# A two-layer encoder trunk on one Trainium2 core: other starting banks, evictions ahead of weight preparations, other memory for summed blocks and evenly spaced convolution taps

## Chip, cores and metric

The kernel runs on one core of one Trainium2 chip. The metric is the device time of one launch in microseconds, as the median of three runs. Five engines work side by side: PE (TensorE, matrix products), DVE (VectorE), ACT (ScalarE), POOL (GpSimd) and SP (SyncE), which here only issues transfers. Each takes its instructions in one fixed order. Products accumulate in banks of a separate memory (PSUM) and are read out of them by DVE or ACT, which the text calls an eviction.

## The reference, cut to what matters

```
for l in range(2):
    h = h + 0.5 * swiglu(rmsnorm(h), w_gate1, w_up1, w_down1)
    h = h + hybrid_mixer(rmsnorm(h), w_in, w_attn_out, conv_w, ..., w_conv_out, w_out)
    h = h + 0.5 * swiglu(rmsnorm(h), w_gate2, w_up2, w_down2)
out = rmsnorm(h)[:, 16:]

def swiglu(x, w_gate, w_up, w_down):
    return (silu(x @ w_gate) * (x @ w_up)) @ w_down

def hybrid_mixer(u, ...):
    q, k, v, a, b, g_sb, g_conv = split(u @ w_in)
    y_sb = stick_breaking_attention(q, k, v) @ w_attn_out
    y_conv = silu(layernorm(depthwise_conv31(a * sigmoid(b)))) @ w_conv_out
    return (sigmoid(g_sb) * y_sb + sigmoid(g_conv) * y_conv) @ w_out
```

All data are float32. There are 528 tokens (512 and 16 learned ones in front), 1024 channels, a feed-forward width of 2816, 8 heads of 64, 512 convolution channels and 31 taps. The last feed-forward stage computes 512 tokens only.

## The kernel before, in words

**Layout.** Channels lie on the 128 partitions and tokens along the free axis; the residual stream is eight tiles `h0` to `h7` of 128x528. A product of 528 columns goes to a bank pair in two halves of 264.

**Precision.** Each operand is split into a rounded high part and the rest: `wh` and `wl` for weights, `uh` and `ul`, `ah` and `al` and so on for activations. Each product is three matmuls (high-high, low-high, high-low). Preparing one weight block is therefore: a DMA into `wr`, a cast on ACT (`wh`, L80) and a subtraction on DVE (`wl`, L81). There are three `wr` buffers, so the DMA of a block starts when the block three places earlier has had its `wl` made. SP issues these transfers in order. `prep_unit` and `unit` (L200 on) run this some units ahead of the products.

**Fewer products by sums.** Two rows of blocks by two columns are multiplied with seven products instead of eight, which needs sums of weight blocks (`s1` to `s4`) and of activation blocks. Sums of raw weights are made partly by accumulating DMAs of POOL (`s<-wg`, `s<-wu`, L209, on top of a block that SP loaded) and partly by adds on DVE (L278). `fetch_sums` loads these blocks into their own tiles.

**Stages.** In each layer: feed-forward 1, mixer, feed-forward 2. Each feed-forward stage computes gate and up in groups of 128 channels, multiplies `silu(gate)` with up (`g`, then `silu` on ACT, then `up`; function `evict`, L669 to L671), splits the result into `ah` and `al`, and after each of four groups adds the down products of these channels: eight products (`down`, L306), of which each is scaled on DVE (`dt`, L803) and added to `h` on POOL (L805). The first feed-forward stage of layer 0 starts in its own way.

**Openings.** The other five stages (three feed-forward, two mixers) begin with `pair`: two sets of seven products interleaved in the order of the table `OPENING`:

```
    OPENING = (("o11", 0), ("o11", 1), ("o21", 0), ("s1", 0), ("s2", 0), ("o21", 1), ("w22", 0), ("s3", 0), ("s1", 1),
               ("s2", 1), ("s4", 0), ("s3", 1), ("w22", 1), ("s4", 1))
```

Each step is 24 matmuls on PE. Its bank tags are `ps` (two banks), `pb` and `pe` (one each); in the mixers their names read `bs`, `bb` and `be`. A step ends with work on other engines: a copy (ACT, L463 and L470), a difference with the kept copy `q` (DVE, L476) or an eviction (`take`). In the feed-forward stages `take` is `evict`; in the mixers it makes the gated convolution input `uc` (L941 to L945). The DVE add behind `s2` and `s4` stands in `prep_unit` (L278), directly ahead of the cast of the sum. After the pair of a feed-forward stage comes its first `down` group. It has four down weights of 512 columns ahead in preparation; its first two products take both `ps` banks, one of which was last used by the last product of the pair.

**The mixer after its pair.** Products `q`, `k`, `v` and the gates (L886) run between the pieces of attention; each half product is evicted on DVE (L986). The 31 taps on four channel tiles (`y`, L911 and L914, 124 instructions a layer) are put behind evictions by `conv_some`: with `CONV_STEP` 5 these are 2 for each evicted half product, and 5 for each call in the pair. What is left of them runs after the first output products of attention.

**Order.** The order on each engine is made by a scheduler from priorities in program order; `with priority(-URGENT)` moves work up, `priority(LATE)` down, and `follow` places a preparation behind the instruction that the products wait for. PE's order in the openings is written out by hand (`manual_schedule`). Memory comes from pools; the summed blocks of a mixer's opening lie in the pool `glu`, whose memory becomes free while the feed-forward stage ahead finishes.

Of the kernel before, what the change touches and what calls it, by code (L numbers as in the profile page):

```python
# [7 lines left out]
F32 = mybir.dt.float32  # L8
# [5 lines left out]
P = 128  # L14
# [47 lines left out]
def kernel(ctx, tc, hT, par, const, wg1, wu1, wd1, win, wao, wco, wout, wg2, wu2, wd2, out):  # L62
# [124 lines left out]

    fetches, later_sums = [], []
# [43 lines left out]
    def fetch_sums(count):  # L232

        for n, name in later_sums[state["sums"]:state["sums"] + count]:
            _, *at = units[n][0]
            if tuple(at[:2]) != quads["of"]:
                return
            state["sums"] += 1
            tag = "s3" if name == "s3" else "s1"
            bufs = 1 if name == "s3" and at[0] == 2 else 2  # L240
            t = quads["pool"].tile([P, 8, P], F32, tag=tag, bufs=bufs, name=tag)
            load(t, n, *{"s1": ("w11", "w12"), "s3": ("w22", "w12")}.get(name, (name,)))
            raws[(name, *at)] = t
# [8 lines left out]
    def prep_unit():  # L252
# [17 lines left out]
        else:  # L270
# [5 lines left out]
            if nk in ("s2", "s4"):  # L276
# [159 lines left out]
    def pair(ptile, sp, st, mode, of, ats, between, take, done):  # L436
# [41 lines left out]

        Bs = [ptile("pb")]
# [5 lines left out]
        for ks in (range(KH - 1), (KH - 1,)):  # L485
            for A, w in zip(As, ws):
                products(A, w, x(0, 0), True, ks)
        begin(Bs[0], v(As[0]))
        copy = ahead["act"]
        between(ptile("pe"), copy)  # L490
        Bs.append(kept(As[1], False))
        G, q, E, c22 = {}, {}, {}, {}

        def step(name, n):
            w = unit(name, *of, ats[n])
            if name == "o21":
                products(As[n], w, x(0, 1))
                take(n, As[n], 0, 0)
# [12 lines left out]
            elif name == "s3":  # L511
# [26 lines left out]
    def rsqrt(r, x, y, ps, n, eps, epscol):  # L538
# [3 lines left out]
        dve.tensor_scalar(out=x, in0=ps, scalar1=1.0 / n, scalar2=eps, op0=ALU.mult, op1=ALU.add)  # L542
# [71 lines left out]
    def ffn(l, fi, st, mode, after):  # L614
# [3 lines left out]
        with tc.tile_pool(name=f"ffn{l}{fi}", bufs=1, reuse_waits="tile") as fp, \  # L618
# [47 lines left out]
            def evict(g, u, c, t):  # L666

                s = toks[t]
                dve.tensor_tensor(out=g[:, s], in0=c[:, 0, :TH], in1=norm["r"][:, s], op=ALU.mult)  # L669
                fn(g[:, s], g[:, s], AF.Silu)  # L670
                dve.tensor_tensor(out=u[:, s], in0=c[:, 1, :TH], in1=g[:, s], op=ALU.mult)  # L671

            def head():
# [9 lines left out]
                def take(n, c, i, t):  # L683
                    if (n, i) not in gu:
                        gu[n, i] = gtile(), fp.tile([P, T], F32, tag="up", bufs=3, name="up")
                    evict(*gu[n, i], c[:, :, :TH], t)
# [99 lines left out]
            def down(gi, opened=False, tp=None):  # L786
# [21 lines left out]
                ws = [unit(f"d{fi}", l, gi, j) for j in ORDER[:2]]  # L808
# [531 lines left out]
```

## Time and profile before

| What | Value |
|---|---|
| median of 3 runs | 2160.44 us |
| the runs | 2160.3, 2160.44, 3285.61 us |
| the profiled execution | 2159.91 us |
| its span, first to last instruction | 2158.1 us |
| matmuls on PE | 16058 |
| mean granted TensorE clock | 0.996 |
| DMA | 334.34 MB |

The profiled execution is 0.5 us below the median, and 1.8 us of it lie outside the span. The profile comes in several views. The page has the busy time of each engine and the chain of work that ended last. The table of waits lists, for one engine, which of its instructions waited, on what, for how long in total, how often, and the longest one. The windows give PE's busy time, the granted clock (PEclk, 1.00 is full) and the share of the DMA engines in stretches of the span. The timeline lists single instructions with start, duration and the idle time before them. Names are those of the program with the buffer numbers left out.

### The profile page before, as it was taken

The page shows a single profiled execution, that of the slowest core. Times are in us where ns is not written, and L with a number is a line of the kernel's source. Part 1 is how long each engine was busy: PE and PEld are TensorE (multiplying, and loading weights), DVE is VectorE, ACT ScalarE, POOL GpSimd, SP SyncE. Part 2 cuts the span into 40 slices and gives each one's busy share as a digit, 9 for nine tenths or more (in the row PEclk, how much of TensorE's full clock was granted, in tenths as well). Part 3 has the DMA queues.
Part 4 walks back from the last instruction along what each step waited for, and adds up shares of the span by engine and source line. Part 5 has one row for each costly group of instructions (what it writes and reads, how often), then busy time and mean ns, then how long its engine had stood idle before and what let it go on. Part 6 is the DMA issues. An engine that isn't in the chain of part 4 may idle for free.

```text
span 2158.1 us, 40005 instructions
## 1 busy us (share of the span) xinstructions
PE 2124.5 (98%) x16058; PEld 2036.0 (94%) x16058; DVE 1595.7 (74%) x2233; ACT 1171.1 (54%) x1660; POOL 512.5 (24%) x477
## 2 busy tenths in 40 slices
PE   9999999999999999999999999999999999999998
PEld 9999999999999999999999999999888888899897
DVE  6867688977766777677787666889777768767685
ACT  6434356577776634343563433466778775444354
POOL 1322321311111231313124222213212112422220
PEclk9999999999999999999999999999999999999999
DMA  7465436765578867464376646358656788665532
GB/s 225 138 166 143 136 104 192 200 137 122 125 178 180 186 160 188 127 160 124 98 189 174 167 134 160 96 171 212 143 127 137 182 186 198 180 172 144 150 106 81
DMA packets 152121, 334.34 MB, mean 155 GB/s; under 512 B 16896, under 2 KB 21120, under 8 KB 151936
## 3 DMA queue, kind: packets, MB, share of 16 engines
q1 hardware_dynamic: 110928, 235.27, 34.3%
q0 software_dynamic: 40320, 95.96, 26.1%
q8 instruction: 126, 2.06, 0.4%
q10 hardware_dynamic: 688, 0.55, 0.1%
q14 instruction: 59, 0.48, 0.1%
HBM read 325.30 MB, written 6.42 MB: 154 GB/s over the span
## 4 chain that ended last, share of the span: by engine, by line
PE 86%; DVE 6%; DMA 4%; ACT 2%; issue 1%; SPq 0%; ACTq 0%; DVEq 0%; POOL 0%; POOLq 0%
PE pb L748 15%; PE ps L748 14%; PE ps L886 13%; PE ps L306 12%; PE ps L872 10%; PE pb L306 6%; PE pe L306 5%; PE pe L748 5%; DVE wl L81 2%; PE z L1068 1%; PE po L1112 1%; ACT wh L80 1%; PE z L1091 1%; DMA wr<-wd 1%; DVE y L914 1%
## 5 line engine op out<-in xcount | busy, mean ns | idle before, releaser
L80 ACT CAST wh<-wr 128x1024 fp32r<-128x1024 f32 (+4 forms) x296 | 263.8, 898 | 353.5 <-PE ps L306 102.1
L81 DVE TENSOR_TENSOR wl<-wr,wh 128x1024 fp32r<-128x1024 f32 (+4 forms) x296 | 326.8, 1107 | 63.2 <-ACT wh L80 60.6
L80 ACT CAST wh<-s 128x1024 fp32r<-128x1024 f32 x171 | 179.4, 1049 | 288.1 <-DVE s L278 108.9
L81 DVE TENSOR_TENSOR wl<-s,wh 128x1024 fp32r<-128x1024 f32 x171 | 233.3, 1365 | 55.8 <-ACT wh L80 55.0
L805 POOL TENSOR_TENSOR h<-h,dt 128x528 f32<-128x528 f32 (+1 forms) x96 | 178.9, 1870 | 262.6 <-DVE dt L803 262.1
L886 PE MATMUL ps<-uh,wh 128*128 128x264 f32 (+1 forms) x664 | 208.0, 313 | 2.7 <-DVE q L986 2.7
L886 PE MATMUL ps<-ul,wh 128*128 128x264 f32 (+1 forms) x664 | 203.7, 307 | 0.0
L886 PE MATMUL ps<-uh,wl 128*128 128x264 f32 (+1 forms) x664 | 203.5, 307 | 0.0
L209 POOL DMA_DIRECT2D s<-wg x81 | 71.8, 886 | 530.9 <-DMA s<-wg 229.5
L914 DVE SCALAR_TENSOR_TENSOR y<-uc,prm,y 128x528 f32<-128x528 f32 (+1 forms) x240 | 186.5, 813 | 0.5
L748 PE MATMUL ps<-ul,wh 128*128 128x264 f32 (+1 forms) x576 | 163.7, 284 | 0.0
L748 PE MATMUL pb<-sl,wh 128*128 128x264 f32 (+1 forms) x576 | 163.3, 283 | 0.0
L748 PE MATMUL ps<-uh,wl 128*128 128x264 f32 (+1 forms) x576 | 163.3, 283 | 0.0
L748 PE MATMUL pb<-sh,wl 128*128 128x264 f32 (+1 forms) x576 | 163.2, 283 | 0.0
L748 PE MATMUL pb<-sh,wh 128*128 128x264 f32 (+1 forms) x576 | 162.9, 283 | 0.0
L748 PE MATMUL ps<-uh,wh 128*128 128x264 f32 (+1 forms) x576 | 162.6, 282 | 0.0
L306 PE MATMUL ps<-ah,wh 128*128 128x264 f32 (+1 forms) x616 | 144.0, 304 | 8.4 <-DVE up L671 8.2
L306 PE MATMUL ps<-al,wh 128*128 128x264 f32 (+1 forms) x616 | 143.8, 304 | 1.0 <-DVE al L81 0.8
L306 PE MATMUL ps<-ah,wl 128*128 128x264 f32 (+1 forms) x616 | 143.4, 303 | 0.0
L263 ACT CAST wh<-wr 128x1024 fp32r<-128x1024 f32 x91 | 95.4, 1049 | 83.0 <-PE ps L886 39.9
L886 PEld LDWEIGHTS ps<-uh,wh 128*128 128x128 f32 x664 | 124.9, 188 | 8.6 <-issue 1.7
L886 PEld LDWEIGHTS ps<-uh,wl 128*128 128x128 f32 x664 | 125.0, 188 | 5.9
(404 smaller groups left out, 6840.1 us busy)
## 6 DMA issues: line engine op xcount, KB each, us to landing
wr<-wd SPq DMA_DIRECT2D x96, 384.0 KB, 3.4
wr<-wg SPq DMA_DIRECT2D x129, 256.0 KB, 3.1
wr<-wu SPq DMA_DIRECT2D x129, 256.0 KB, 3.6
wr<-win SPq DMA_DIRECT2D x56, 512.0 KB, 3.9
wl<-win POOLq DMA_DIRECT2D x54, 512.0 KB, 7.9
s<-wg SPq DMA_DIRECT2D x87, 256.0 KB, 4.5
s<-wu SPq DMA_DIRECT2D x87, 256.0 KB, 5.3
s<-wg POOLq DMA_DIRECT2D x81, 256.0 KB, 5.3
```

Of the source, the lines that this page charges most:

```text
L80: i = act.copy(hi, x)
L81: return i, dve.tensor_tensor(out=lo, in0=x, in1=f(hi), op=ALU.subtract)
L209: queue.dma_start(raw[:, a:b], src, **kw)
L263: act.copy(hi[:, :nk], raw[:, :nk])
L306: pe.matmul(ps[:, c, :n], wt[:, k0 + k, :], xt[:, s:s + n], start=(k == 0 and pi == 0), stop=(k == end and pi == 2))
L748: pe.matmul(ps[:, e, :TH], wt[:, 4 * e + kk, :], xt, start=start and kk == 0 and pi == 0, stop=kk == 3 and pi == 2, skip_group_check=True)
L805: pool.tensor_tensor(out=tri(h[j], mode), in0=tri(h[j], mode), in1=tri(t, mode), op=ALU.add)
L872: pe.matmul(ps, wt[:, k0 + k, :], xt[:, s], start=(n == 0 and pi == 0), stop=(n == nk - 1 and pi == 2))
L886: pe.matmul(ps, wt[:, k, :], xt[:, s], start=(n == 0 and pi == 0), stop=(n == KD - 1 and pi == 2))
L914: t = dve.scalar_tensor_tensor(out=y, in0=uc[i][:, c0 + k:k + T], scalar=col(w0 + k), in1=y, op0=ALU.mult, op1=ALU.add)
L1068: pe.matmul(z[:, hh, :n], kk[r, ks], qq[r, q0:q0 + n], start=(pi == 0), stop=False, skip_group_check=True)
L1091: pe.matmul(z[:, hh, pq - q0:pq - q0 + pn], onesm, s[:, hh, :], start=False, stop=False, skip_group_check=True)
```

## The change

Seven edits, all in the openings and their surroundings:

1. **The first down group of an opened feed-forward stage** (`down`): three products begin together, in the banks `ps`, `pb` and `pe`, instead of two in the two `ps` banks. None of the three was used by the last product of the pair.
2. **Evictions first** (`out` in `pair`, `done`): most evictions of the pair, and the split of their results, run under `priority(-URGENT)`, and the preparations of weights are told to follow them.
3. **The add for `s4`** (`add_w21`): it leaves `prep_unit` and is issued two steps of the pair or more ahead, at the steps `("w22", 0)` and `("s4", 0)`.
4. **The start of the pair**: the first two products interleave by their inner blocks in the pattern 0-2, 0-1, 3, 2-3, so the first of them ends six matmuls earlier.
5. **Summed blocks**: their tiles are allocated in the reverse of the order in which they are loaded, and in the mixers they come from a pool of their own (`gls`).
6. **Taps**: none is placed in the pair or behind the first `q`; behind each other half product there are 2.5 on average (a credit is carried over).
7. **Constants** of the mixer are staged in `gls` too.

```diff
@@ pair
+        def out(n, c, i, t):
+            with priority(-URGENT):
+                ahead["act"], ahead["dve"] = take(n, c, i, t)
+
...
-        for ks in (range(KH - 1), (KH - 1,)):
-            for A, w in zip(As, ws):
-                products(A, w, x(0, 0), True, ks)
+        for n, ks in ((0, (0, 1, 2)), (1, (0, 1)), (0, (3,)), (1, (2, 3))):
+            products(As[n], ws[n], x(0, 0), True, ks)
...
+        def add_w21(n):
+            x, y = raws[("s1", *of, ats[n])], raws[("w21", *of, ats[n])]
+            dve.tensor_tensor(out=x, in0=x, in1=y, op=ALU.add)
+
         def step(name, n):
+            if (name, n) in (("w22", 0), ("s4", 0)):
+                add_w21(int(name == "s4"))
             w = unit(name, *of, ats[n])
             if name == "o21":
                 products(As[n], w, x(0, 1))
-                take(n, As[n], 0, 0)
+                (out if n else take)(n, As[n], 0, 0)
...
                 opposite(c22[n], Bs[n], q[n])
-                take(n, c22[n], 1, 1)
+                out(n, c22[n], 1, 1)
             elif name == "w22":
                 products(E[n], w, sx(3))
-                take(n, E[n], 1, 0)
+                out(n, E[n], 1, 0)
             else:
                 done(n, 1)
                 products(Bs[n], w, x(1, 1))
-                with priority(-n * URGENT):
-                    take(n, Bs[n], 0, 1)
+                out(n, Bs[n], 0, 1)
                 done(n, 0)
@@ prep_unit
-            if nk in ("s2", "s4"):
+            if nk == "s2" or nk == "s4" and at not in opened:
@@ done, in the head of a feed-forward stage
                     if i:
-                        while late:
-                            parts(*late.pop())
-                        parts(u, ms[n] + 1)
+                        with priority(-URGENT):
+                            while late:
+                                parts(*late.pop())
+                            parts(u, ms[n] + 1)
@@ down
-                ws = [unit(f"d{fi}", l, gi, j) for j in ORDER[:2]]
-                pds = [ptile() for j in range(2)]
+                ws, pds = [], []
+                if opened:
+                    tags = ("ps", "pb", "pe", "ps")
+                n0 = 3 if opened else 2
+                for n in range(n0):
+                    state["look"] = LOOK - n * opened
+                    ws.append(unit(f"d{fi}", l, gi, ORDER[n]))
+                    pds.append(ptile(tags[n]))
+                state["look"] = LOOK
                 with tc.manual_schedule(engines={mybir.EngineType.PE}) if opened else nullcontext():
                     for ks in (range(nk - 2), (nk - 1,), (nk - 2,)):
-                        for j in range(2):
+                        for j in range(n0):
                             gemm(pds[j], ws[j], 0, nk, xs, mode, ks, nk - 2)
@@ fetch_sums
+        some = []
         for n, name in later_sums[state["sums"]:state["sums"] + count]:
...
+            if units[n][0][1:3] == quads["of"]:
+                some.append((n, name))
+        state["sums"] += len(some)
+        for n, name in some[::-1]:
             tag = "s3" if name == "s3" else "s1"
...
+            raws[(name, *units[n][0][1:])] = quads["space"].tile([P, 8, P], F32, tag=tag, bufs=bufs, name=tag)
+        for n, name in some:
+            load(raws[(name, *units[n][0][1:])], n, *{"s1": ("w11", "w12"), "s3": ("w22", "w12")}.get(name, (name,)))
@@ mixer
-                conv_some(CONV_STEP * sum(s.stop - s.start for _, s in outs) // HALF // 2, i)
+                conv_some(CONV_STEP * sum(s.stop - s.start for _, s in outs) / T, i)
...
             def conv_some(n, behind):
+                credit[0] += n
                 with priority(LATE):
-                    while n and todo and (todo[0][0] | 1) < len(uc):
+                    while credit[0] >= 1 and todo and (todo[0][0] | 1) < len(uc):
...
-                    conv_some(CONV_STEP, last_evac[0])
...
-                quads.update(pool=glu, of=(2, l))
+                quads.update(pool=glu, space=gls, of=(2, l))
                 if l == 0:
-                    constants(glu)
+                    constants(gls)
...
-                                conv_some(CONV_STEP * (c.stop - c.start) // HALF // 2, ev)
+                                if name != "q" or i:
+                                    conv_some(CONV_STEP * (c.stop - c.start) / T, ev)
```

The change moves instructions at three places that matter here. The first is PE at the first down group of feed-forward 2 in layer 0 (its twins in layer 1 read alike). `ps_9583`, `ps_9584` and `pb_9642` are down products, `ah_9531`, `ah_9408`, `ah_9535` and `ah_9567` the high parts of the four activation blocks, the last of which comes from the last eviction of the pair. Before:

```order
L306 MATMUL ps_9583<-ah_9408,wl_9455 128x264 x2
L306 MATMUL pb_9642<-ah_9531,wh_9525 128x264 x2
L306 MATMUL pb_9642<-al_9532,wh_9525 128x264
L306 MATMUL ps_9584<-ah_9531,wh_9492 128x264 x2
L306 MATMUL ps_9584<-al_9532,wh_9492 128x264 x2
L306 MATMUL ps_9584<-ah_9531,wl_9493 128x264 x2
```

Now, with `ah_9571` as the block from the last eviction:

```order
L308 MATMUL ps_9581<-ah_9413,wl_9459 128x264 x2
L308 MATMUL pb_9582<-ah_9535,wh_9496 128x264 x2
L308 MATMUL pb_9582<-al_9536,wh_9496 128x264 x2
...
L308 MATMUL pe_9583<-ah_9535,wh_9529 128x264 x2
L308 MATMUL pe_9583<-al_9536,wh_9529 128x264 x2
...
L308 MATMUL pe_9583<-ah_9539,wl_9530 128x264 x2
L308 MATMUL ps_9581<-ah_9571,wh_9458 128x264 x2
```

Before, 15 matmuls stood between the last product of the pair and the first matmul into the bank that this product had used (`ps_9584`). Now no bank of the three is that one, and 54 matmuls stand ahead of the first that reads `ah_9571`.

The second place is DVE in the same opening, from the step `w22` of the first set to the `s3` of the second. `s_9015` and `s_9014` hold the block that is added for `s4`. Before:

```order
L669 TENSOR_TENSOR g<-c_9327,rstd 128x264
L278 TENSOR_TENSOR wr<-wr,s_9015 128x1024
L671 TENSOR_TENSOR up<-c_9327,g 128x264
L81 TENSOR_TENSOR wl<-wr,wh 128x1024
L81 TENSOR_TENSOR wl<-s_9223,wh 128x1024
L476 SCALAR_TENSOR_TENSOR pe<-ps,q 128x264
L81 TENSOR_TENSOR al<-up,ah 128x528
L476 SCALAR_TENSOR_TENSOR pe<-ps,q 128x264
L81 TENSOR_TENSOR wl<-wr,wh 128x1024
L278 TENSOR_TENSOR s_9116<-s_9116,s_9297 128x1024
L669 TENSOR_TENSOR g<-pb,rstd 128x264
L81 TENSOR_TENSOR wl<-s_9116,wh 128x1024
```

Now, from the place of the add on `wr`:

```order
L680 TENSOR_TENSOR g<-ps,rstd 128x264
L502 TENSOR_TENSOR wr<-wr,s_9014 128x1024
L682 TENSOR_TENSOR up<-ps,g 128x264
L81 TENSOR_TENSOR wl<-wr,wh 128x1024
...
L680 TENSOR_TENSOR g<-c_9332,rstd 128x264
L502 TENSOR_TENSOR s_9120<-s_9120,s_9302 128x1024
L682 TENSOR_TENSOR up<-c_9332,g 128x264
...
L680 TENSOR_TENSOR g<-pb,rstd 128x264
L682 TENSOR_TENSOR up<-pb,g 128x264
L81 TENSOR_TENSOR wl<-s_9120,wh 128x1024
```

The add on `wr` went from the eviction of `c` to the first eviction of the pair (`g<-ps`), and the second add took its old place; where the second add was, the eviction of `pb` now runs through without it.

The third place is DVE at the end of the pair of the mixer in layer 0, from the last gated input `uc` to the first `k`. Before:

```order
L942 TENSOR_TENSOR uc_4817<-bs,rstd 128x264
L914 SCALAR_TENSOR_TENSOR y_5045<-uc_4855,prm,y_5045 128x528
L914 SCALAR_TENSOR_TENSOR y_5043<-uc_4709,prm,y_5043 128x528
...
L986 SCALAR_TENSOR_TENSOR q<-ps,rstd 128x264
L914 SCALAR_TENSOR_TENSOR y_5043<-uc_4709,prm,y_5043 128x528
```

Now:

```order
L964 TENSOR_TENSOR uc_4820<-bs,rstd 128x264
L1008 SCALAR_TENSOR_TENSOR q<-ps,rstd 128x264 x2
L81 TENSOR_TENSOR ql<-q,qh 128x528
L1008 SCALAR_TENSOR_TENSOR k<-ps,rstd 128x264
L932 TENSOR_SCALAR y_5229<-uc_4712,prm 128x528
```

Five taps stood between the last `uc` and the first `q`, and four behind it; both halves of `q` now come directly behind the last `uc`, and the taps start behind the first half of `k`.

More of the change, by code (lines that the diff above doesn't have):

```diff
@@ L185, in pieces @@
         return [(0, nk, src[:, :nk])]
+    quads["space"] = None
     fetches, later_sums = [], []
@@ L232, in fetch_sums @@
     def fetch_sums(count):
+        some = []
         for n, name in later_sums[state["sums"]:state["sums"] + count]:
[L235 to L238, printed above, removed]
+            if units[n][0][1:3] == quads["of"]:
+                some.append((n, name))
+        state["sums"] += len(some)
+        for n, name in some[::-1]:
             tag = "s3" if name == "s3" else "s1"
[L240 to L243, printed above, removed]
+            bufs = 1 if name == "s3" and units[n][0][1] == 2 else 2
+            raws[(name, *units[n][0][1:])] = quads["space"].tile([P, 8, P], F32, tag=tag, bufs=bufs, name=tag)
+        for n, name in some:
+            load(raws[(name, *units[n][0][1:])], n, *{"s1": ("w11", "w12"), "s3": ("w22", "w12")}.get(name, (name,)))
     ahead = {}
@@ L541, in rsqrt @@
         fn(r, r, AF.Exp, bias=B_ZERO, scale=-0.5)
-        dve.tensor_scalar(out=x, in0=ps, scalar1=1.0 / n, scalar2=eps, op0=ALU.mult, op1=ALU.add)
+        ahead["rstd"] = dve.tensor_scalar(out=x, in0=ps, scalar1=1.0 / n, scalar2=eps, op0=ALU.mult, op1=ALU.add)
         dve.tensor_tensor(out=y, in0=r, in1=r, op=ALU.mult)
@@ L668, in evict @@
                 s = toks[t]
-                dve.tensor_tensor(out=g[:, s], in0=c[:, 0, :TH], in1=norm["r"][:, s], op=ALU.mult)
-                fn(g[:, s], g[:, s], AF.Silu)
+                i = dve.tensor_tensor(out=g[:, s], in0=c[:, 0, :TH], in1=norm["r"][:, s], op=ALU.mult)
+                j = fn(g[:, s], g[:, s], AF.Silu)
                 dve.tensor_tensor(out=u[:, s], in0=c[:, 1, :TH], in1=g[:, s], op=ALU.mult)
+                return j, i
             def head():
@@ L685, in take @@
                         gu[n, i] = gtile(), fp.tile([P, T], F32, tag="up", bufs=3, name="up")
-                    evict(*gu[n, i], c[:, :, :TH], t)
+                    return evict(*gu[n, i], c[:, :, :TH], t)
                 def done(n, i):
@@ L805, in update @@
                     pool.tensor_tensor(out=tri(h[j], mode), in0=tri(h[j], mode), in1=tri(t, mode), op=ALU.add)
-                ws = [unit(f"d{fi}", l, gi, j) for j in ORDER[:2]]
-                pds = [ptile() for j in range(2)]
+                ws, pds = [], []
[7 more added lines that the diff above has]
+                state["look"] = LOOK
                 with tc.manual_schedule(engines={mybir.EngineType.PE}) if opened else nullcontext():
                     for ks in (range(nk - 2), (nk - 1,), (nk - 2,)):
-                        for j in range(2):
+                        for j in range(n0):
                             gemm(pds[j], ws[j], 0, nk, xs, mode, ks, nk - 2)
-                for n in range(2):
+                for n in range(n0):
                     update(ORDER[n], pds[n])
-                for n, j in list(enumerate(ORDER))[2:]:
+                for n, j in list(enumerate(ORDER))[n0:]:
                     if last and after is finish_prepare and n == KD - 2:
@@ L916, in conv_some @@
                         tc.add_manual_dep(t.ins, behind.ins.name, NOSYNC, reason="convolution in the gaps")
-                        n -= 1
+                        credit[0] -= 1
             with tc.tile_pool(name=f"glu{l}", bufs=1, reuse_waits="tile") as glu, \
+                    tc.tile_pool(name=f"gls{l}", bufs=1, reuse_waits="tile") as gls, \
                     tc.tile_pool(name=f"psg{l}", bufs=1, space=bass.MemoryType.PSUM, reuse_waits="tile") as psg:
@@ L943, in take @@
                                                      op=ALU.mult)
-                    fn(x[:, a:b], x[:, a:b], AF.Sigmoid)
+                    i = fn(x[:, a:b], x[:, a:b], AF.Sigmoid)
                     pool.tensor_tensor(out=y[:, PAD + a:PAD + b], in0=y[:, PAD + a:PAD + b], in1=x[:, a:b], op=ALU.mult)
-                    conv_some(CONV_STEP, last_evac[0])
+                    return i, last_evac[0]
                 def done(n, i):
```

4 lines of the change are left out of this document (2 added, 2 removed).

## The prediction, made before the changed kernel was run

> **What bounds the kernel now.** I read the page first, for the engine that is never idle.
>
> ```profile
> span 2158.1 us, 40005 instructions
> PE 2124.5 (98%) x16058; PEld 2036.0 (94%) x16058; DVE 1595.7 (74%) x2233; ACT 1171.1 (54%) x1660; POOL 512.5 (24%) x477
> ```
>
> PE is busy for 98% of the span, so 2158.1 - 2124.5 = 33.6 us of idle time is all that an edit to waits can give, plus whatever the clock costs. The number of matmuls stays. Next comes the table of PE's waits over the whole span (total, times, longest).
>
> ```profile
> PE ps L306 <- DVE up L671: 8.2, 3, 3.2
> PE ps L886 <- DVE q L986: 2.7, 2, 1.5
> PE ps L457 <- DVE up L671: 1.6, 1, 1.6
> PE pe L457 <- DVE pe L476: 1.4, 2, 0.9
> PE pb L457 <- DVE wl L81: 1.3, 2, 0.6
> PE ps L306 <- DVE al L81: 0.8, 2, 0.4
> PE bb L457 <- DVE wl L81: 0.8, 1, 0.8
> PE bs L457 <- ACT bb L470: 0.4, 2, 0.2
> ```
>
> All eight kinds lie in openings, which the windows of PE around the five confirm (length, busy time, clock, share of the DMA engines).
>
> ```profile
> 364.00:420.00 56.00, 52.98 (x427) 1.00 0.79 205
> 742.00:815.00 73.00, 68.91 (x534) 0.95 0.66 172
> 1087.00:1165.00 78.00, 73.23 (x580) 0.98 0.77 195
> 1449.00:1510.00 61.00, 59.21 (x460) 1.00 0.83 218
> 1798.00:1870.00 72.00, 67.04 (x462) 1.00 0.76 193
> ```
>
> They miss 3.0, 4.1, 4.8, 1.8 and 5.0 us, together 18.6. The rest of the idle time is at the start and the end of the program, where nothing is edited. Two windows also have a lower clock. So I looked at the chain of waits around the three first down groups (start, duration, what).
>
> ```profile
> 764.49 1.15 DVE s L278
> ...
> 769.69 5.97 DMA wr<-wd
> ...
> 775.76 0.63 ACT wh L80
> ...
> 777.50 7.35 PE ps L306 x36
> ```
>
> Before 777.50 PE waits for a bank. The bank is freed by the last eviction, whose `silu` stands on ACT behind the cast of the fourth down weight (775.76), and that weight landed at 769.69 + 5.97 = 775.66. Behind the wait 36 matmuls take 7.35 us. Elsewhere 36 of this shape take 4.38; the second row is the twin in layer 1.
>
> ```profile
> 149.50 4.38 PE pb L306 x36
> ...
> 1140.81 6.17 PE ps L306 x36
> ```
>
> The excess is 2.97 and 1.79 us, together 4.8, and the windows give the reason.
>
> ```profile
> 777.00:783.00 6.00, 5.50 (x25) 0.50 0.91 200
> 1142.00:1144.00 2.00, 2.00 (x11) 0.50 1.13 206
> 1847.00:1850.00 3.00, 3.00 (x15) 1.00 1.10 232
> ```
>
> The granted clock fell to half behind the first two waits and stayed full behind the third, the longest one. The cost in reach is therefore 17.2 us of waits (the sum of the table above) and 4.8 us of slow clock, 22.0 in all.
>
> **Three banks at the first down group (waits of 8.2 and 0.8, clock 4.8).** The edit does not make the last eviction earlier. The cast of the fourth weight still stands ahead of the last `silu`, and the fourth transfer still waits for the first `wl`. It gives PE other work meanwhile: 54 matmuls instead of 15 stand ahead of the first one that reads the last activation block. At 4.38/36 = 0.1217 us each they last 6.57 us. Whether that suffices is read from these rows of the timeline: the first down matmul of each of the three places and the last `al`.
>
> ```profile
> 772.41 0.40 PE L306 MATMUL ps<-ah,wh 128*128 128x264 f32 x2
> 778.14 0.71 DVE L81 TENSOR_TENSOR al<-up,ah 128x528 fp32r<-128x528 f32 x1 [0.70 <-ACT ah L80]
> 1136.16 0.40 PE L306 MATMUL ps<-ah,wh 128*128 128x264 f32 x2
> 1141.45 0.71 DVE L81 TENSOR_TENSOR al<-up,ah 128x528 fp32r<-128x528 f32 x1 [0.70 <-ACT ah L80]
> 1840.54 0.39 PE L306 MATMUL ps<-ah,wh 128*128 128x512 f32 x1
> 1847.22 0.69 DVE L81 TENSOR_TENSOR al<-up,ah 128x512 fp32r<-128x512 f32 x1 [0.69 <-ACT ah L80]
> ```
>
> In layer 0 PE reaches the block at 772.41 + 6.57 = 778.98 and needs `al` two matmuls later, at 779.22; `al` ends at 778.85, 0.37 us ahead. In layer 1 it is 1142.97 against 1142.16, 0.81 ahead. At the last place, with half as many matmuls of 512 columns (27 at 0.1217 x 2 x 512/528 = 0.236), it is 1840.54 + 6.37 + 0.24 = 1847.15 against 1847.91, 0.76 late. This assumes that the fourth transfer is issued when it is now. Two things move its issue against each other. The add at 764.49 (1.15 us), now the head of that chain, leaves it; one eviction and one `al` of about 0.7 move ahead of the first `wl`. I take them as even. Of 8.2 us I leave 1.0 (the 0.76 and something), so 7.2 go; the ends are 0, if the transfer comes over 2 us later, and 8.2. Of the 0.8 for `al` ahead of the group I take 0.4 (ends 0 and 0.8). The 4.8 of slow clock should go whole: the mixer window 364-420 holds waits up to 1.5 at a clock of 1.00, and what I expect to remain is shorter. Its ends are 0 and 4.8.
>
> **Evictions first and the earlier add (waits of 1.6, 1.4 and 1.3 in the pair).** Here an eviction stands behind a preparation that waits for a transfer, on ACT or DVE:
>
> ```profile
> 744.72 1.05 ACT L80 CAST wh<-s 128x1024 fp32r<-128x1024 f32 x1 [1.99 <-DMA s<-wu]
> 746.13 0.43 DVE L671 TENSOR_TENSOR up<-ps,g 128x264 f32<-128x264 f32 x1 [2.11 <-ACT g L104]
> 1105.18 8.00 DMA s<-wu
> ```
>
> In the first two rows a cast waits 1.99 us for a summed block, `silu` stands behind it, `up` behind `silu`, and the difference that PE reads (`pe`, L476) behind `up`. In the new order `silu` stands ahead of the cast. The third row is the accumulating transfer of 8.00 us behind the wait of 1.6. Its preparation stays ahead of `up`, but the eviction's first half and the add do not stand between them any more, which are 0.4 and 1.1 us of the 1.6. The `pb` waits of 0.6 come from an add directly ahead of the cast; it is now made more than ten DVE instructions earlier. Of 4.3 us I take 3.3. The ends are 4.3 and a loss: each add now waits for its block ahead of evictions, so a block that lands late holds DVE and what is queued behind it. Its load is among the first of the opening, so I set this end at -2, a quarter of the 8.00.
>
> **Taps, blocks and the start of the pair in the mixers (2.7, 0.8 and 0.4).** The first `q` is evicted behind five taps:
>
> ```profile
> 415.00 4.44 DVE L914 SCALAR_TENSOR_TENSOR y<-uc,prm,y 128x528 f32<-128x528 f32 x5
> 419.37 0.42 DVE L986 SCALAR_TENSOR_TENSOR q<-ps,rstd 128x264 f32<-128x264 f32 x1
> ```
>
> Without them `q` has 4.4 us more than it needs, so the 2.7 go. The wait of 0.8 on `wl` hung on summed blocks that are now loaded while the stage before still runs, and the 0.4 on a copy that comes six matmuls (0.7 us) earlier. Of 3.9 I take 3.3 (ends 2 and 3.9).
>
> **What it adds.** The taps do not vanish. In two stretches of 20 us they now take the following on DVE (second number), and in the stretches behind them DVE as a whole and PE are busy so:
>
> ```profile
> 410.00:430.00 20.00, 15.82 (x21) 1.00 0.94 240
> 1495.00:1515.00 20.00, 16.79 (x23) 1.00 0.98 247
> ...
> 430.00:630.00 200.00, 153.99 (x246) 1.00 0.59 135
> 1515.00:1705.00 190.00, 143.57 (x219) 1.00 0.62 138
> ...
> 430.00:630.00 200.00, 199.86 (x1605) 1.00 0.59 135
> ```
>
> The first two rows are of the taps alone, the next two of all DVE work, the last of PE. The 15.8 and 16.8 us move into the stretches behind, where DVE is idle for 46 and 46 us; 30 remain. That idle time covers them. If none of it did, they would cost 32.6 us. PE is busy for 199.86 of 200 us there, so it waits for none of DVE's work now, and I take the near end, 1.0. The summed blocks of the mixers are loaded between the last down weights, and one of POOL's accumulations now waits for its block ahead of the scaling of the last `up`. I put 1.0 on it (ends 0 and 4, half of the 8.00 above).
>
> **The sum.** 7.2 + 0.4 + 4.8 + 3.3 + 3.3 = 19.0, less 2.0, is a gain of 17.0 us. The profiled execution took 2159.9, which gives 2142.9; the median stands 0.5 higher, so the forecast is **2143.4**.
>
> **Rivals.**
>
> *The slow clock comes back.* The half rate shows behind waits of 2.75 and 2.27 us and not behind 3.20, so a wait alone does not decide it. If something else in these stretches does, the 4.8 us return: 2148.2. For it speaks that the longest wait kept the clock; against it that both drops begin right behind a wait. The Trainium skill, page "TensorE: Matmul & The Clock Gate", section "Part 1: The HAM clock gate (the "warmup" mystery)", has the clock fall to half after at least one idle window of about 3.4 us, counted by a free-running counter. By that rule none of the three waits was long enough, the two slow stretches would not be theirs, and this rival's time would be the result; the trace disagrees as far as the drops sit on two waits shorter than that. 12%.
>
> *The fourth down weight lands later.* Its issue now follows two more DVE instructions, and the DMA engines are full there (0.91 to 1.13 in the windows above). If it takes the 8.00 us of the slowest transfer instead of 5.97, the last `al` is late by 8.00 - 5.97 - 0.37 = 1.7 in layer 0, and with the same 2.03 by 1.2 and 2.8 in layer 1. That is 5.7 instead of 1.0, and stalls of this size can halve the clock again: 2143.4 + 4.7 + 4.8 = 2152.9. Against it: blocks that were queued just ahead of it are now loaded earlier. 17%.
>
> *The openings are paced by transfers.* Then PE waits at the next place for what it no longer waits for here. All that stays is the mixers' 3.3 less 2.0: 2160.4 - 1.3 = 2159.1. For it speaks the DMA share of 0.76 to 0.83 in four of the five windows; against it that seven of the eight waits name an order on DVE or ACT. 9%.
>
> *Slower: the moved taps come out uncovered.* Behind each half product of `k`, `v` and the gates DVE then has 2.5 taps instead of 2, and both attention and the next half product queue behind them. The price is up to 32.6 us, and it decides from 18 us on, which is 55% of the moved time. At two thirds it is 21.7: 2160.4 - 18.0 + 21.7 = 2164.1. Against it stand 46 us of idle DVE time in each stretch, and a PE that now waits for 0.14 us in the first of them. 4%.
>
> **How the numbers follow.** The forecast has 58%, with a range of its own of 2139 to 2149: the end below is all 22.0 us and no cost (2160.4 - 22.0 = 2138.4), the end above the first rival. The rivals take 42% together. Cutting off the slower one, half of the paced one and the last bit below leaves 8 in 10 between 2138 and 2157. A change of 2% is 43 us, about what a measurement of this kernel tells from no change. The largest gain here is 22.0 and the largest loss 32.6, so within 2% is nearly certain: 0.985, with 0.005 for faster and 0.01 for slower, for what I have not seen.
>
> **What would show it.** In the profile after, the table of PE's waits should have no bank wait at the first down groups and at most 1 us for `al` there; the 36 matmuls behind should take 4.4 us at a clock of 1.00; `q` should be gone from the table; the five windows should miss some 6 us instead of 18.6. A new line of waits on `sl`, `k` or `gs` between 430 and 630 would show the taps. I am wrong in the mechanism if the bank waits stay, or if the down groups wait for a weight.

## The result, and the profile after

The changed kernel takes 2142.47 us (median of four runs, 2140.82 to 2145.03) against 2162.31 for the kernel before on the same chip. The ratio is 0.9912, with a 95% interval of 0.9893 to 0.9932: some 19 us less, which is inside 2%. The run of 3285.61 us of the kernel before is left out of this comparison. The profiled execution took 2141.3 us. Its page begins with the span and the engines.

```profile
span 2139.5 us, 39983 instructions
PE 2118.2 (99%) x16058; PEld 2031.1 (95%) x16058; DVE 1600.1 (75%) x2233; ACT 1170.8 (55%) x1660; POOL 514.1 (24%) x477
```

The number of matmuls is the same. PE is busy for 6.3 us less (2124.5 to 2118.2) and idle for 12.3 us less (33.6 to 21.3), together the 18.6 us of the span. The table of PE's waits shows where the idle time went (total, times, longest).

```profile
PE ps L761 <- DVE dt L816: 1.6, 2, 0.8
PE ps L308 <- ACT ah L80: 1.5, 3, 0.9
PE ps L308 <- DVE al L81: 0.9, 3, 0.4
PE bs L459 <- DVE wl L81: 0.9, 1, 0.9
PE ps L906 <- DMA wl<-win: 0.7, 2, 0.4
PE bs L459 <- ACT bb L472: 0.5, 2, 0.3
```

The first row of the table (4.7 us at the program's start), those on `h` and `nt` (0.5, 0.4 and 0.4) and one of 0.2 are left out. The bank wait of 8.2 us (`ps` on `up`, at the first down products) is gone, and so are `q`, `pe` and `pb`. The row on `dt` is new. The five openings lie a little earlier now; their windows, up to 6 us shorter than those of before, are (length, PE busy, clock, DMA share):

```profile
361.00:417.00 56.00, 55.24 (x450) 1.00 0.59 159
739.00:806.00 67.00, 66.21 (x544) 1.00 0.70 185
1080.00:1156.00 76.00, 74.65 (x608) 1.00 0.76 198
1441.00:1498.00 57.00, 55.31 (x425) 1.00 0.61 162
1782.00:1848.00 66.00, 64.45 (x441) 1.00 0.82 216
```

They miss 0.8, 0.8, 1.35, 1.7 and 1.55 us, together 6.1 instead of 18.6 (a wait of 0.3 us for `win`, at 417.7, stands just behind the first window), and the clock is full in all five. In the chain of waits the first opened down group of layer 0 is a run of matmuls; below it stand the transfers of the fourth down weight that the chain passes through in layer 1.

```profile
776.40 5.86 PE ps L308 x48
...
791.01 2.95 PE ps L761 x24
...
794.00 0.60 DVE dt L816
...
1120.54 7.15 DMA wr<-wd
...
1822.21 6.93 DMA wr<-wd
```

The 48 matmuls take 5.86 us, 0.122 each, which is the undisturbed rate. The rows at 791.01 and 794.00 are the new wait: 24 matmuls of the next group, then PE stands until DVE has made `dt`. The timeline of PE gives what is left at the three places (the wait is in brackets):

```profile
794.74 0.36 PE L761 MATMUL ps<-sh,wh 128*128 128x264 f32 x1 [0.79 <-DVE dt L816]
1130.20 0.51 PE L308 MATMUL ps<-ah,wh 128*128 128x264 f32 x2 [0.24 <-ACT ah L80]
1130.94 0.52 PE L308 MATMUL ps<-al,wh 128*128 128x264 f32 x2 [0.23 <-DVE al L81]
1831.62 0.50 PE L308 MATMUL ps<-ah,wh 128*128 128x512 f32 x1 [0.94 <-ACT ah L80]
1832.35 0.50 PE L308 MATMUL ps<-al,wh 128*128 128x512 f32 x1 [0.22 <-DVE al L81]
```

Layer 0 has no wait for the last block, layer 1 has 0.47 us, and the last place 1.16. DVE and PE in the stretch that took the moved taps, DVE in the first row:

```profile
430.00:630.00 200.00, 164.89 (x262) 1.00 0.60 134
430.00:630.00 200.00, 199.86 (x1605) 1.00 0.60 134
```

DVE has 10.9 us more to do there than before (153.99) and PE is as busy as it was.

### The profile page after: what moved, and what is told of

It reads as the page before. It is cut to its first block, busy times and chain, and to the rows that moved or that the text cites. A ratio compares the mean times of both kernels' runs of the same rounds, so it can differ in the third digit from the quotient of the medians.

```text
span 2139.5 us, 39983 instructions
## 1 busy us (share of the span) xinstructions
PE 2118.2 (99%) x16058; PEld 2031.1 (95%) x16058; DVE 1600.1 (75%) x2233; ACT 1170.8 (55%) x1660; POOL 514.1 (24%) x477
## 4 chain that ended last, share of the span: by engine, by line
PE 88%; DVE 5%; DMA 4%; ACT 1%; issue 1%; POOL 0%; SPq 0%; DVEq 0%; ACTq 0%; POOLq 0%
PE ps L761 15%; PE pb L761 14%; PE ps L906 13%; PE ps L308 11%; PE ps L892 10%; PE pb L308 6%; PE pe L308 5%; PE pe L761 5%; DMA wl<-win 1%; DVE wl L81 1%; PE ps L459 1%; PE z L1091 1%; PE po L1135 1%; PE z L1114 1%; PE bb L459 1%
## 5 line engine op out<-in xcount | busy, mean ns | idle before, releaser
L81 DVE TENSOR_TENSOR wl<-wr,wh 128x1024 fp32r<-128x1024 f32 (+4 forms) x296 | 331.5, 1124 | 64.8 <-ACT wh L80 62.3
```

Source lines behind the costliest of these rows:

```text
L81: return i, dve.tensor_tensor(out=lo, in0=x, in1=f(hi), op=ALU.subtract)
```

## The experiments

The kernel before took 2162.31 to 2167.80 us (medians) beside the different runs, so each kernel is compared by its ratio to the kernel before on the same chip. The changed kernel itself was timed twice: 0.9912 above and 0.9899 in its repetition.

| run | what it is | us | ratio, 95% interval |
|---|---|---|---|
| e1 | change with two starting banks | 2155.22 | 0.9943 (0.9928 to 0.9958) |
| e2 | before with three starting banks | 2153.2 | 0.9936 (0.9921 to 0.995) |
| e10 | before, last eviction ahead of the fourth weight's cast | 2148.81 | 0.9915 (0.9901 to 0.993) |
| e8 | change with two banks, longer last eviction | 2154.07 | 0.9946 (0.9928 to 0.9965) |
| e11 | the change again | 2143.37 | 0.9899 (0.9884 to 0.9913) |
| e9 | change, last eviction first, two banks swapped | 2136.83 | 0.9871 (0.9856 to 0.9886) |
| e13 | as e9, but two starting banks | 2138.62 | 0.9875 (0.9861 to 0.989) |
| e4 | change with the old order of evictions and adds | 2145.01 | 0.9909 (0.9893 to 0.9926) |
| e5 | change with the blocks in the old memory | 2150.98 | 0.9937 (0.9918 to 0.9957) |
| e3 | change with the old taps | 2142.66 | 0.9903 (0.9886 to 0.992) |
| e6 | change without 30 of the 31 taps | 2140.24 | 0.9891 (0.9872 to 0.991) |
| e0 | the kernel before, profiled on another chip | 2163.84 | 1.0005 (0.9992 to 1.0018) |

### The banks, taken back and alone

```diff
-                if opened:
-                    tags = ("ps", "pb", "pe", "ps")
-                n0 = 3 if opened else 2
+                n0 = 2
                 for n in range(n0):
-                    state["look"] = LOOK - n * opened
```

> The changed kernel with its first down groups begun on the two ps banks again, all other edits kept. Theory (the bank waits and the slow clock behind them are one cause, worth 11 to 12 us of the 19): the wait of the first down matmuls on the last up comes back at the three feed-forward openings, 6 to 9 us in total, at least one of them with a stretch at half clock behind it, and the time is 2150 to 2156 us. Rival (the gain comes from the order of evictions and adds, and the slow clock is not tied to the waits): no more than 3 us of bank waits, and 2147 us or less.

The table of waits and three windows of PE in this kernel:

```profile
PE ps L308 <- DVE up L682: 11.8, 3, 4.3
```

```profile
775.00:780.00 5.00, 5.00 (x31) 0.68 0.32 77
1135.00:1140.00 5.00, 4.67 (x21) 0.50 0.57 153
1840.00:1845.00 5.00, 4.47 (x11) 0.50 0.43 101
```

The bank wait is back at all three places (3.67, 4.28 and 3.89 us). That is longer than in the first profile of the kernel before, more than the 6 to 9 us in all that were expected, and shorter than in a second profile of the kernel before, shown below. Behind each of them the granted clock is low. Between 0.9943 and the change's 0.9899 to 0.9912 lie 7 to 10 us. So in this kernel the three banks carry between a third and a half of the gain, clock included.

The second kernel does the other half of the test: the kernel before with only the hunk of the function `down`.

> The kernel before with the three starting banks alone. Theory: the bank waits of 8.2 us and both half-clock stretches go, at most 2.5 us of waits for the last activation block come in their place, the waits inside the pair (4.3 us) and on q (2.7 us) stay; 2148 to 2152 us. Rival (the cover is long enough only with the evictions moved up too): waits of over 4 us remain at the down groups, with a half-clock stretch, 2155 us or more.

```profile
PE pe L457 <- DVE pe L476: 3.2, 2, 2.6
PE ps L893 <- DVE q L993: 2.8, 2, 1.9
PE ps L748 <- DVE dt L803: 1.5, 2, 0.8
```

No wait for a bank at the down groups is left. The waits of the pair and of `q` stay, and one of `dt` has come, as in the change: it belongs to the banks' edit. No slow clock is left at the down groups; one stretch of it has come behind a wait for `q` of 1.87 us, told in the last section. 0.9936 is 14 us.

### Is it the banks, or the order on ACT?

The prediction had the last `silu` standing on ACT behind the cast of the fourth weight. If that order is the cause, moving the cast behind the eviction should do without a third bank. In the kernel before:

```diff
-                split(raw[:, :nk], hi[:, :nk], lo[:, :nk])
+                pair_ = split(raw[:, :nk], hi[:, :nk], lo[:, :nk])
+                if state.get("hold"):
+                    for i, engine in zip(pair_, ("act", "dve")):
+                        follow(i, engine)
...
-                        parts(*late.pop())
+                        ahead["act"], ahead["dve"] = parts(*late.pop())
...
-                ws = [unit(f"d{fi}", l, gi, j) for j in ORDER[:2]]
+                state["hold"] = opened
+                ws = [unit(f"d{fi}", l, gi, ORDER[0])]
+                state["hold"] = False
+                ws.append(unit(f"d{fi}", l, gi, ORDER[1]))
```

The first hunk is in `prep_unit`: while `hold` is set, the fourth weight's cast and difference follow what is noted in `ahead`, the split of the last activation block.

> The kernel before, still with two starting banks, where the preparation of the fourth down weight is placed behind the last eviction and its split on ACT and DVE, instead of ahead of them. Theory (the bank wait is a wait for the fourth weight's transfer, passed on by the order on ACT): without that order the last up is ready within 0.5 us of PE's need, the bank waits shrink from 8.2 to under 1.5 us and both half-clock stretches go; 2147 to 2152 us. Rival (the last eviction is late by itself, since DVE and ACT are full there): at least 4 us of the bank waits stay, 2154 us or more.

```profile
PE ps L309 <- DVE up L675: 0.7, 2, 0.3
```

The bank wait falls to 0.7 us with the two banks of before, and no clock drop is left. 0.9915 is 18 us: this one edit of order gives about what the whole change gives. The same edit on the changed kernel, once with three starting banks (the banks of the seventh and eighth products swapped as well, against the `dt` wait) and once with two:

```diff
-                    tags = ("ps", "pb", "pe", "ps")
+                    tags = ("ps", "pb", "pe", "ps", "ps", "pb", "ps", "pe")
...
+                    state["hold"] = opened and n == 0
                     ws.append(unit(f"d{fi}", l, gi, ORDER[n]))
+                    state["hold"] = False
...
-                    pd = ptile(tags[n % 4])
+                    pd = ptile(tags[n % len(tags)])
```

> The changed kernel with two more edits: the fourth down weight is prepared behind the last eviction and its split, and the seventh and eighth down products swap banks, so that the last one is not in ps, which the next stage needs. Theory (what is left there is the order on ACT and the bank of the last product): both waits on dt (1.6 us) and all on the last activation block (1.5 and 0.9 us) go, 3 to 5 us faster than the changed kernel beside it. Rival (PE then waits for the fourth weight itself, whose preparation now comes last): a new wait of PE on a down weight of 2 us or more, no faster.

> The changed kernel with two starting banks again and the fourth down weight prepared behind the last eviction and its split. Theory (the three banks hide a wait that the order on ACT makes, and with the other order there is nothing to hide): bank waits under 1 us in all, no wait on dt, no half-clock stretch, 2 to 4 us faster than the changed kernel beside it. Rival (the three banks are worth something by themselves, since the last eviction is late anyway): bank waits of 2 us or more, and slower than the changed kernel by 2 us or more.

> The changed kernel once more, so that the next three have it beside them. Every theory: 0.988 to 0.994 of the time of the kernel before, no bank wait on up at the down groups, a wait of 0.8 us on dt behind two of them, and between 1 and 4 us on the last activation block.

In the first of them the chain of waits runs through the end of the group that had the `dt` wait:

```profile
791.44 5.85 PE ps L765 x48
797.30 2.82 PE pb L765 x23
```

48 matmuls follow without a stop where the change stood still after 24. This kernel is 6.5 us faster than the change beside it (2136.83 against 2143.37), and the fastest of the study. That is more than the 3 to 5 us that were expected. Part of it lies outside the edit: in the profiled execution of the change PE waited for 1.79 us up to 59.8 us, ahead of every opening, and lost clock behind that; here it waited for 0.41 at that place. With two banks it is 2138.62, and the ratios 0.9871 and 0.9875 have intervals that overlap almost wholly. Once the order on ACT is right, no gain of the third bank can be measured.

### The clock, by a longer wait and by the kernel before

```diff
+                for _ in range(more):
+                    act.copy(g[:, s], g[:, s])
                 j = fn(g[:, s], g[:, s], AF.Silu)
```

The start is the kernel of two banks; `more` is 5 for the last eviction of the pair and 0 elsewhere.

> The changed kernel with two starting banks, and with five copies of the last gate half on itself on ACT ahead of its silu (nothing is computed differently), so that the bank waits grow by about 2 us each to 3.5 to 5.5 us. Theory (the wait halves the clock behind it, and a wait longer than all of those before does so at each place): three half-clock stretches, each worth 1.5 to 3 us, 2160 to 2168 us. Rival (where the drop falls does not hang on the length of the wait): at least one place keeps its clock at 1.00; about 2157 us.

The wait did not become longer but changed its kind: the order put matmuls of another product ahead, which wait for the fourth weight's cast.

```profile
PE pe L308 <- ACT wh L80: 5.4, 3, 2.4
PE ps L308 <- DVE up L684: 2.5, 2, 1.5
```

Waits of 1.01 and 1.54 us in layer 0 kept the clock, 2.02 and 0.92 in layer 1 and 2.37 at the last place lost it. So there is no wait of the length that was wanted, and length alone does not sort those that there are; the last section returns to them. A second profile of the kernel before says more.

> The kernel before once more with a profile, on another chip than the first. Theory (its spread from chip to chip is how late the fourth down weight lands, passed on to the bank waits and to the clock): 2163 to 2170 us, bank waits of 9 to 12 us in all instead of 8.2, and half-clock stretches behind all three of them. Rival (the spread is elsewhere): the same time, with bank waits of 8.2 us and two stretches as before.

The fourth weight's transfer in the chain of waits, and three windows of PE:

```profile
767.77 7.73 DMA wr<-wd
...
1133.72 8.35 DMA wr<-wd
...
1841.31 8.36 DMA wr<-wd
```

```profile
778.00:784.00 6.00, 6.00 (x32) 0.58 0.42 100
1144.00:1150.00 6.00, 6.00 (x34) 0.64 0.45 107
1853.00:1856.00 3.00, 3.00 (x11) 0.69 0.28 90
```

The same kernel, and each transfer is 1.7 to 2.9 us longer than in the profile that the prediction read (5.97, 5.49, 6.64). The bank waits are 4.51, 5.10 and 4.92, and now all three places lose clock, the last one too. They are longer by 1.76, 2.83 and 1.72 us, and the transfers by 1.76, 2.86 and 1.72: PE waits longer by what the transfer takes longer. The bank wait is thus the wait for this transfer, handed on by the order on ACT. The first profile showed a favourable execution: there these places cost 8.2 us of waits and 4.8 of slow clock, 13.0 in all, here 14.5 and, by an estimate from the stretches at half clock (776.25 to 783.08, 1141.48 to 1148.31 and 1851.45 to 1854.86, half of PE's busy time in them), 6.8, some 21 in all. So a cure of these places alone can be worth the 18 us above.

### The order of evictions, the memory and the taps, each taken back

In e4 the evictions of the pair and the adds stand as before:

```diff
-            with priority(-URGENT):
-                ahead["act"], ahead["dve"] = take(n, c, i, t)
+            with priority(-URGENT * (n == 1 and i == 0 and t == 1)):
+                take(n, c, i, t)
...
-            if (name, n) in (("w22", 0), ("s4", 0)):
-                add_w21(int(name == "s4"))
```

> The changed kernel with the order of evictions, splits and adds in the pair as before (the three banks, the blocks and the taps stay). Theory (these orders are worth the 4.3 us of waits inside the pair): waits on pe, wl and up inside the pairs of 3 to 6 us come back, and the time is 3 to 6 us above the changed kernel's. Rival (the three banks alone cannot cover a later eviction): in addition over 3 us of waits at the down groups, with a half-clock stretch, 8 us or more above it.

```profile
PE pb L459 <- DVE wl L81: 1.4, 2, 0.8
PE ps L459 <- DVE up L680: 0.4, 1, 0.4
```

1.8 us of the pair's 4.3 came back (the repetition of the change has 0.3 of them, on `pb`, itself), not the whole, and the wait of `pe` stayed away. The time rose by 1.6 us over the change beside it, within the intervals. In e5 only the memory of the summed blocks and of the mixer's constants and the order of the blocks' allocation are as before:

```diff
-        for n, name in some[::-1]:
+        for n, name in some:
...
-                quads.update(pool=glu, space=gls, of=(2, l))
+                quads.update(pool=glu, space=glu, of=(2, l))
                 if l == 0:
-                    constants(gls)
+                    constants(glu)
```

> The changed kernel with the summed blocks and the mixer's constants in the memory of before, allocated in the order of their loads (three banks, the order of evictions and the taps stay). With the order of evictions put back alone, only 1.8 of the 4.3 us of waits inside the pairs had returned. Theory (the waits of 1.6 and 1.4 hang on blocks that land late, and either edit alone removes most of them): 1 to 2.5 us of waits on wl, up and pe inside the pairs, 0.5 to 1 us of them in the mixers, 0 to 3 us above the changed kernel. Rival (the memory is what removed them): 3 us or more of these waits, 3 to 6 us above it.

```profile
PE ps L308 <- ACT ah L80: 5.2, 3, 2.2
PE bs L459 <- DVE wl L81: 1.2, 1, 1.2
PE pe L459 <- DVE pe L478: 0.8, 1, 0.8
...
PE pb L459 <- DVE wl L81: 0.5, 1, 0.5
PE ps L459 <- DVE wl L81: 0.5, 1, 0.5
```

0.9937 against 0.9899 to 0.9912: some 5 to 8 us are lost, which neither expectation put at the place where the profile has it. Of the waits for `ah`, 1.17 and 2.24 us stand at opened down groups, behind transfers of the fourth weight of 7.86 and 8.20 us, and the second takes the clock along. (The third, 1.83, is at 59.5 us, before any opening, and takes the clock along too; the repetition of the change has one of 1.79 there that does the same, so it makes no difference between the two.) The waits of the pair come back in part (0.8, 0.5 and 0.5). Whether the old memory makes those transfers longer, or they were long by chance in this execution, stays open.

Of the taps, e3 puts back the old places and e6 leaves out 30 of 31 (240 instructions of DVE):

```diff
-                                if name != "q" or i:
-                                    conv_some(CONV_STEP * (c.stop - c.start) / T, ev)
+                                conv_some(CONV_STEP * (c.stop - c.start) // HALF // 2, ev)
```

> The changed kernel with the taps where they were: in the pair, behind the first q, and 2 for each half product. Theory (the taps' only price before was the wait on q): the waits on q come back with 2 to 3.5 us, no other does, and the time is 2 to 4 us above the changed kernel's. Rival (the denser taps behind cost something that no wait of PE shows): no slower than the changed kernel, within 1 us.

> The changed kernel without 30 of the 31 taps of the convolution: it leaves out 240 DVE instructions of 0.8 us, some 190 us of DVE work. Theory (all of them are covered by products): PE's waits between 430 and 630 stay at 0.1 us, and the time is that of the changed kernel within 2 us. Rival (the moved taps cost time behind the openings): 3 us faster or more.

With the old taps, the wait for `q`:

```profile
PE ps L906 <- DVE q L1009: 0.4, 1, 0.4
```

Without the 30 taps, so with a result that is not the convolution's, DVE and PE are busy in the stretch behind the opening as follows:

```profile
430.00:630.00 200.00, 79.03 (x143) 1.00 0.60 135
430.00:630.00 200.00, 199.87 (x1607) 1.00 0.60 135
```

The first expectation fell: 0.4 of the 2.7 us returned, and 0.9903 is the change's own ratio. The second held: with 86 us less for DVE to do in that stretch PE is busy for 0.01 us more. Its 0.9891 is 1 to 4 us below the change's ratios, with intervals that overlap. So no cost of the taps is seen where they are now, and almost none where they were, once the evictions ahead of them are early.

## Why the prediction was right, and where it was not

The forecast was 2143.4 with a range of 2138 to 2157; the result is 2142.47. The main step was right and was shown: PE stands at the down groups because the last eviction waits on ACT for the fourth weight, and 54 matmuls cover all but 1.6 us of this. Point by point:

**Bank waits, 7.2 of 8.2.** 7.0 by the trace: 0.24 and 0.94 us on `ah` are left. The working can be followed further. In layer 1 the transfer took 7.15 us instead of 5.49; less the 0.81 of spare time, this is 0.85 late, and 0.47 was seen. At the last place the 0.76 that were forecast, 0.29 of longer transfer and 0.41 from an issue that comes later against the first down product make 1.46, and 1.16 was seen. The assumption that the issue does not move was right within 0.5 us: it came 2.72, 2.68 and 2.42 us ahead of the first down product in the three places of before, and 2.73 and 2.01 ahead of it in the last two now. Of the wait on `al`, 0.4 was to go; 0.45 at the groups instead of 0.36 is 0.1 more, and 0.45 of the 0.8 was at 58.8 us, in no opening, against the sentence that all eight kinds lie there.

**Slow clock, 4.8 whole.** Right. PE's busy time fell by 6.3 us, no stretch inside the program is below 1.00, and with the waits back (two banks) the drops came back at all three places. The reason that was given, that what remains is shorter than a wait of 1.5 which kept the clock, holds as well; why the longest wait of before kept it is told in the last section.

**Pair, 3.3 of 4.3.** All of `pe`, `pb` and `ps` on `up` went, 4.3. But the reason that was given holds for part of it: taking the order back returned 1.8, and taking the memory back, which the sum had counted only for the mixers, returned 1.8 as well (0.8, 0.5, 0.5).

**Mixers, 3.3 of 3.9.** 2.5 went: `q` whole (2.7), while 0.8 on `bb` in layer 0 went and 0.9 on `bs` in layer 1 came, whose preparation now stands behind the evictions of `c` and `uc`, and the 0.4 on the copy is 0.5. That `q` waited because of five taps was wrong as a sole cause. With those taps back it waits for 0.4.

**Costs, 1.0 and 1.0.** The taps show no cost. Waits of 0.9 us for `win` are new, but the kernel before with three banks, which has none of the edits to the blocks, has one of 0.5 too, so nothing shows that the earlier blocks make them.

**Not foreseen, 1.6.** The banks of the opened group now alternate by a list of four, so its eighth product sits in the `ps` bank that the second product of the next group wants. Its `dt` stands on DVE behind the add of two weight blocks, 0.8 us late in both layers. The prediction counted matmuls up to the first bank that is reused, and did not go on to the end of the list. The run with the list of eight names removes the wait.

These terms make 7.0 - 0.1 + 4.8 + 4.3 + 2.5 - 0.9 - 1.6 = 16.0 of the 18.6 us. 1.5 us more of PE's busy time and 1.1 us of idle time are not accounted for. The time came out right with errors on both sides of the sum, so its closeness, 0.9 us, is in part luck; the mechanism is not.

Of the rivals, the slow clock did not return without waits. The fourth weight's transfer did take longer in layer 1 (by 1.66 and 0.29 us), but not by the 2.03 that the rival took. That it did not is partly luck: with no edit at all it took 1.72 to 2.86 us longer in the second profile of the kernel before, and the run with the old memory shows what the rival described, a transfer of 8.20 us, a wait of 2.24 and a slow clock. The openings are not paced by transfers, since they miss 6.1 us and not some 17. The taps are covered, so the slower rival falls. What the prediction had in hand and did not use is the cheaper cure: it named the cast ahead of the last `silu`, and that order alone, turned round, is worth 18 us on the kernel before.

## What to carry to other kernels

Where an engine waits for a bank, follow the wait to the instruction that releases it and ask what stands ahead of that on its own queue; if it is a preparation that waits for a transfer, turn that order round before buying cover with more buffers. A buffer's name given to one product is taken from a later one: go through the new assignment up to the next group that wants it. An edit whose term is small, here the memory of some blocks, is worth a run of its own: it carried 5 to 8 us of the 19.

## What the runs showed of the hardware

The granted clock falls behind waits of PE, but not by one length. Every wait at a down group of 3.67 us or more took it to half for some microseconds. Between 1.8 and 3.2 us both happen: it fell behind 1.87, 2.20, 2.24, 2.27, 2.37 and 2.75 and stayed behind 2.41, 2.59 and 3.20. A wait of 1.79, one of 1.83 and one of 2.02, each with a shorter one close behind, took it down too; behind a single wait below 1.7 it stayed.

The traces show what decides: where the wait lies on a grid of time. In the second profile of the kernel before the clock falls at 776.25, 1117.58, 1141.48 and 1851.45 us and, behind the last matmul, at 2158.65. The steps between these are 100, 7, 208 and 90 times 3.413 us, and in every other profile with more than one fall the steps are whole multiples of it too. Cut into windows of this grid, the first three rows below are from the kernel before with three banks (a wait of 1.87, then one of 2.59 in two windows), the last two from the first profile of the kernel before (the wait of 3.20). PE's idle time is the first number less the second.

```profile
417.63:421.04 3.41, 1.54 (x13) 1.00 1.05 276
1806.85:1810.27 3.42, 2.38 (x20) 1.00 1.02 214
1810.27:1813.68 3.41, 1.86 (x16) 1.00 1.07 237
1841.69:1845.10 3.41, 1.70 (x8) 1.00 1.04 275
1845.10:1848.52 3.42, 1.93 (x8) 1.00 1.12 232
```

The first window is idle for 1.87 us and the clock falls at its end; 1.04 and 1.55, 1.71 and 1.49 leave it full. From 12 us to the last matmul, the 14 profiles hold 15 such falls, each at the end of a window with 1.87 us or more of idle time, and no window at full clock with 1.71 or less was followed by one. So a wait of 3.20 that a grid line cuts in half keeps the clock, and one of 1.87 inside a window loses it. The slow stretch then lasted one window where PE's idle time in it was at most 0.41 us and two where it was 0.77 or more: the falls at 776.73 and 1141.95 in the first profile of the kernel before are of the two kinds, which gives the 2.97 and 1.79 us of the prediction. The grid lies differently in each execution, so a wait between 1.9 and some 3.5 us (an estimate, twice the bound of 1.71 to 1.87) costs clock in one and not in another.

The Trainium skill, page "TensorE: Matmul & The Clock Gate", section "Part 1: The HAM clock gate (the "warmup" mystery)", has the clock fall after at least one idle window of about 3.4 us of a free-running counter. The grid of 3.413 us agrees with it; that the window must be idle as a whole does not, since thirteen of the 15 falls followed windows that were idle for 1.87 to 3.15 us.

The transfer of the fourth down weight (256 KB) into full DMA engines took between 5.49 and 8.36 us at the same three places of the same kernel in two executions, and in layer 1 it was 5.49 in the one and 8.35 in the other. A cover that is counted from one profile, as the 54 matmuls of 6.57 us were, has to allow for that.
